# A hybrid encoder layer on one core: the second k tile's modulation on VectorE, statistics ahead of normalising, and the first gating later in the program

## The chip, the cores and the metric

The kernel runs on one core of a Trainium2 chip. The metric is the device time of one execution in microseconds; of the kernel before, three runs gave a median of 936.51 us (934.34 to 937.18). The engines are named as in the profile: PE is TensorE, DVE is VectorE, ACT is ScalarE, POOL is GpSimd, SP is SyncE, which here only issues transfers. PEld is TensorE's loading of weights, which runs beside its products.

## The reference

One layer (DEPTH 1, batch 1, 512 tokens, width 2048). A conditioning vector gives shift, scale and gate; the normalised stream is modulated, projected once onto 7168 columns, and the columns feed a spatial gating group and a neighbourhood attention group:

```python
mod = jax.nn.silu(c) @ w_ada[l] + b_ada[l]
shift, scale, gate = jnp.split(mod[:, None, :], 3, axis=-1)
h = _layernorm(x) * (1.0 + scale) + shift
proj = h @ w_in[l]
u, v, z_a, q, k, v_b, z_b = jnp.split(proj, IN_SPLITS, axis=-1)
y_a = _spatial_gating(gelu(u), gelu(v), z_a, ...)      # u * (W_s LN(v) + b) * silu(z_a)
y_b = _neighbourhood_attention(q, k, v_b, rpb) * silu(z_b)
y = jnp.concatenate([y_a, y_b], axis=-1) @ w_out[l]
x = _layernorm(DEEPNORM_ALPHA * x + (1.0 + gate) * y, ln_g[l], ln_b[l])
```

The gating normalises v in groups of 128 channels, multiplies by a gain and adds a bias per channel, mixes the 128 positions of each chunk with W_s, adds a bias, and multiplies by u and silu(z_a).

## The kernel before

**Products.** Every float32 product is made of three products of rounded parts: the activations are split into h_hi and h_lo, the weights into whi and wlo (`mm3`, L224; `mm_vz`, L237). ACT makes the high part of a weight tile (`L194`), and DVE or POOL subtracts it from the raw tile to get the low part (`L196`); which of the two engines does it is the last field of an entry of the plan (`plan_group`). Weight tiles are read ahead on SP's queue through four raw buffers.

**The start.** The 512 tokens are four tiles of 128 rows (xt). For each, DVE takes statistics (`bn_stats`, `bn_aggr`, L428, L429), POOL makes the factor of the normalisation (L430 to L433), then the four quarters of 512 columns are normalised (L437 on ACT, L440 on POOL or DVE), TensorE transposes each (L444) and ACT copies it back (L445). In the list `LASTS` the fourth tile's quarters stand between the steps of the modulation. The width of 2048 is 16 k tiles of 128. A k tile can be used in products when its shift and scale (modc) are known. For k tiles 0 and 1 these come from TensorE, 32 one-column products each (`ada_tensor`, L348), and DVE adds the bias (L352). For the other 14, in pairs, DVE runs through the weights with a multiply-add into PSUM (`ada_vector`, L363 and L365; acc_ps holds the sums), one addition joins the two halves (L371), and TensorE sums over the partitions with a column of ones (`ada_end`, L379, L380). `make_h` then makes h_hi (ACT, L392) and h_lo (DVE, L393, L397).

**The first part of the projection** is done in segments of k tiles while the modulation proceeds; each segment goes through five groups of columns: VZ0 (first quarter of v_b and z_b), V, U, ZA (half of v, u and z_a) and KQ0. Four banks of PSUM stay with VZ0 throughout; the others are emptied into sums in SBUF (`sum_evac`). The last segment (`last_segment`, k tiles 12 to 15) goes in the order of its list, KQ0, V, U, VZ0, ZA, and empties each group on DVE (L755), with a Gelu or Silu on ACT (L759, L762) and, for ZA, one more product on DVE (L760).

**The first gating** (`sgu`) runs beside the last segment: `run(main, side, pace, start)` takes steps of `side` between the steps of `main`, one for every `pace` steps from step `start` on, and the rest at the end. Its steps for each of four tiles of v are: statistics (L547, L548), the inverse root on POOL (`rsqrt_var`, L120 and L121); then the normalisation on DVE (L552) and two multiplications or additions of 128x512 on POOL (L554, L555). Four steps with TensorE products (L561) and two DVE operations (L562, L565) follow. Its gain, bias, W_s and b_s are loaded on ACT's queue into the four quarters of y_b[1].

**After it** come three groups (qi = 1 to 3) of quarters of v_b, z_b, k and q (`project`, four banks turning with a fifth), each with the attention of the quarter before it as its side (`PACES`), whose scores and values use the PSUM ring "x". v_lo (L688) is made where an attention begins; values (L680 to L682) need the low parts of L710. gate1, which holds the gate later, is filled with zeros by POOL (L530) and its bias loaded ahead of the gating.

**What sets the order** is the order in which instructions are recorded, arranged by a scheduler engine by engine; on each engine it is fixed.

Of the kernel before, what the change touches and what calls it, by code (L numbers as in the profile page):

```python
# [1 line left out]

# [13 lines left out]
P = 128  # L16
D = 2048
T = 512
# [19 lines left out]
            ([4, 5], [VZ0, V, U, ZA, KQ0]), ([6, 7], [KQ0, V, U, VZ0, ZA])]  # L38
# [8 lines left out]
PACE_FIRST = (1.5, 19)  # L47
PACES = [(1.2, 2.95), (1.2, 3.15), (1.2, 3.3), (1.2, 3.15)]
# [11 lines left out]
def run(main, side, pace=1, start=0):  # L60
# [5 lines left out]
    for _ in side:  # L66
        pass
# [3 lines left out]
def hybrid_kernel(ctx: ExitStack, tc: tile.TileContext, x, c, w_ada, b_ada_cols, b_gate, w_in,  # L71
# [235 lines left out]

    with tc.tile_pool(name="ph1", bufs=1) as ph1:
# [65 lines left out]
        def ada_end(k0):

            pc = bank()[:, :4].rearrange("p (s k) -> p s k", s=2)
            for s in range(2):
                for i in range(2):
                    nc.tensor.matmul(pc[:, s, i:i + 1], lhsT=scratch[1][:, (2 * s + i) * P:(2 * s + i + 1) * P], rhs=one, start=True, stop=True)  # L379
            nc.vector.tensor_tensor(out=modc[:, :, k0:k0 + 2], in0=pc, in1=bada[:, :, k0:k0 + 2], op=ALU.add)  # L380
# [37 lines left out]
        nb = ph1.tile([P, NT], F32, name="nb")  # L418
# [4 lines left out]
        def first_norm(n):  # L423

            xn = xt[:, n, :]
            st = ph1.tile([P, 4, 6], F32, name="st", tag="st", bufs=2)
            for i in range(4):
                nc.vector.bn_stats(out=st[:, i, :], in_=xn[:, i * 512:(i + 1) * 512])  # L428
            nc.vector.bn_aggr(out=mv[:, n, :], in_=st)  # L429
            nc.gpsimd.tensor_scalar(out=mv[:, n, 0:1], in0=mv[:, n, 0:1], scalar1=-1.0, scalar2=0.0, op0=ALU.mult, op1=ALU.add)  # L430
            nc.gpsimd.tensor_scalar(out=rstd[:, n:n + 1], in0=mv[:, n, 1:2], scalar1=1.0, scalar2=EPS, op0=ALU.mult, op1=ALU.add)
            nc.gpsimd.tensor_tensor(out=rstd[:, n:n + 1], in0=rstd[:, n:n + 1], in1=mhalf[:, 0:1], op=ALU.pow)
            nc.gpsimd.tensor_scalar(out=nb[:, n:n + 1], in0=mv[:, n, 0:1], scalar1=rstd[:, n:n + 1], scalar2=0.0, op0=ALU.mult, op1=ALU.add)  # L433
            for q in range(4):
                cs = slice(q * T, (q + 1) * T)
                if q == 1:
# [548 lines left out]
```

## Time and profile before

| what | value |
|---|---|
| median of three runs | 936.51 us (934.34 to 937.18) |
| the profiled execution, its span | 936.44 us, 934.7 us |
| busy share PE, DVE, ACT, POOL | 95%, 64%, 35%, 36% |
| mean granted TensorE clock | 0.976 of full |

The span is the time from the first to the last instruction in the profile; the profiled execution's own time is 1.74 us longer. A row of a timeline gives the start, the time that the group of equal instructions took, the engine, the line of the kernel, the operation and the tiles; an entry in square brackets is the time the engine stood idle before it and what ended the wait.

### The profile page before, as it was taken

To read this page: it belongs to the slowest core of one execution; us is meant where nothing else is said; L and a number is where in the kernel's file an instruction comes from. 1 tells how busy PE (TensorE), PEld (TensorE's weight loads), DVE (VectorE), ACT (ScalarE), POOL (GpSimd) and SP (SyncE) were. 2 spreads that over 40 slices of the span, in tenths; PEclk is the share of its full clock that TensorE was granted. 3 is DMA by queue.
4 is the path that set the end of the run, shared out by engine and by line. 5 is a ranking of instruction groups with operands and counts; after the bars stand their busy time and mean duration, and the time that the engine had idled before them with its cause. 6 is when DMAs were issued, how large, how long until landed. Compare 5 with 4: busy or idle time off the path is not lost.

```text
span 934.7 us, 11916 instructions
## 1 busy us (share of the span) xinstructions
PE 890.4 (95%) x4528; PEld 775.7 (83%) x4528; DVE 596.9 (64%) x827; ACT 324.0 (35%) x401; POOL 339.0 (36%) x246
## 2 busy tenths in 40 slices
PE   3899899999997999999999999999999999999993
PEld 3888688888886898899889988999888888888883
DVE  5055898854485544686759686877868835252667
ACT  4235333322614152543345153625154511212300
POOL 4235554635573241615261624253256000000035
PEclk9679999999998999999999999999999999999997
DMA  9778888853422332344543554543333292323213
GB/s 301 220 242 289 276 295 263 292 168 124 143 72 90 91 100 77 117 135 122 176 152 121 164 167 138 158 152 122 113 111 112 91 353 97 113 92 112 90 60 121
DMA packets 107787, 145.59 MB, mean 156 GB/s; under 512 B 6994, under 2 KB 78802, under 8 KB 106962
## 3 DMA queue, kind: packets, MB, share of 16 engines
q1 hardware_dynamic: 103120, 134.25, 45.1%
q10 hardware_dynamic: 4610, 10.59, 3.2%
q8 instruction: 35, 0.57, 0.3%
q14 instruction: 22, 0.17, 0.1%
HBM read 140.62 MB, written 4.19 MB: 155 GB/s over the span
## 4 chain that ended last, share of the span: by engine, by line
PE 82%; POOL 4%; DVE 4%; issue 4%; DMA 3%; SPq 1%; ACT 1%; POOLq 0%; DVEq 0%; ACTq 0%
PE psm L224 52%; PE psx L224 15%; PE psm L237 8%; DMA wada<-in_w_ada_dram 2%; SPq L320 1%; POOL wlo L196 1%; PE ada L348 1%; POOL xr L864 1%; DVE s L552 1%; PE psx L682 1%; PE psx L634 1%; PE psx L633 1%; PE psx L680 1%; DMA xt<-in_x_dram 1%; POOL xr L865 1%
## 5 line engine op out<-in xcount | busy, mean ns | idle before, releaser
L194 ACT CAST whi<-raw 128x1024 fp32r<-128x1024 f32 x133 | 139.2, 1049 | 337.5 <-PE psm L224 216.9
L196 DVE TENSOR_TENSOR wlo<-raw,whi 128x1024 fp32r<-128x1024 f32 x94 | 131.4, 1399 | 160.8 <-ACT whi L194 155.2
L224 PE MATMUL psm<-h_hi,whi 128*128 128x512 f32 x444 | 175.1, 395 | 0.0
L224 PE MATMUL psm<-h_lo,whi 128*128 128x512 f32 x444 | 173.7, 391 | 0.0
L224 PE MATMUL psm<-h_hi,wlo 128*128 128x512 f32 x444 | 173.2, 390 | 0.0
L196 POOL TENSOR_TENSOR wlo<-raw,whi 128x1024 fp32r<-128x1024 f32 x39 | 95.0, 2443 | 107.4 <-ACT whi L194 83.8
L224 PE MATMUL psm<-whi,h_hi 128*128 128x512 f32 (+1 forms) x296 | 114.7, 388 | 0.0
L224 PE MATMUL psm<-wlo,h_hi 128*128 128x512 f32 (+1 forms) x296 | 114.0, 385 | 0.0
L224 PE MATMUL psm<-whi,h_lo 128*128 128x512 f32 (+1 forms) x296 | 114.0, 385 | 0.0
L224 PEld LDWEIGHTS psm<-h_hi,wlo 128*128 128x128 f32 x444 | 83.3, 188 | 17.8
L224 PEld LDWEIGHTS psm<-h_hi,whi 128*128 128x128 f32 x444 | 84.0, 189 | 15.2
L224 PEld LDWEIGHTS psm<-h_lo,whi 128*128 128x128 f32 x444 | 83.9, 189 | 15.1
L237 PE MATMUL psm<-whi,h_hi 128*128 128x256 f32 x248 | 71.4, 289 | 4.0 <-ACT whi L194 2.1
L237 PE MATMUL psm<-wlo,h_hi 128*128 128x256 f32 x248 | 71.3, 288 | 0.2 <-POOL wlo L196 0.2
L121 POOL TENSOR_TENSOR rs<-vareps,mhalf 128x1 f32<-128x1 f32 x4 | 4.4, 1098 | 184.4 <-DVE vareps L120 184.4
L237 PE MATMUL psm<-whi,h_lo 128*128 128x256 f32 x248 | 70.9, 287 | 0.1
L224 PEld LDWEIGHTS psm<-wlo,h_hi 128*128 128x128 f32 x296 | 63.6, 215 | 8.5
L224 PEld LDWEIGHTS psm<-whi,h_lo 128*128 128x128 f32 x296 | 63.4, 214 | 8.5
L224 PEld LDWEIGHTS psm<-whi,h_hi 128*128 128x128 f32 x296 | 63.4, 214 | 8.4
L365 DVE SCALAR_TENSOR_TENSOR ada<-wada,c_sb,ada 128x512 f32<-128x512 f32 x91 | 64.0, 749 | 7.4 <-DMA wada<-in_w_ada_dram 3.9
L224 PE MATMUL psx<-h_hi,whi 128*128 128x512 f32 x160 | 64.5, 403 | 4.1 <-ACT whi L194 2.2
L224 PE MATMUL psx<-h_hi,wlo 128*128 128x512 f32 x160 | 63.5, 397 | 2.9 <-POOL wlo L196 2.9
(199 smaller groups left out, 1679.6 us busy)
## 6 DMA issues: line engine op xcount, KB each, us to landing
wada<-in_w_ada_dram SPq DMA_DIRECT2D x128, 256.0 KB, 5.5
raw<-in_w_in_dram SPq DMA_DIRECT2D x128, 256.0 KB, 3.2
raw<-in_w_in_dram SPq DMA_DIRECT2D x48, 512.0 KB, 4.2
rawg<-in_w_ada_dram SPq DMA_DIRECT2D x32, 512.0 KB, 4.1
raw<-in_w_out_dram SPq DMA_DIRECT2D x32, 512.0 KB, 3.6
xt<-in_x_dram SPq DMA_DIRECT2D x8, 512.0 KB, 8.6
xr<-in_x_dram ACTq DMA_DIRECT2D x4, 1024.0 KB, 9.4
tt<-in_rpb_dram ACTq DMA_DIRECT2D x16, 128.0 KB, 2.9
```

What stands on the lines that cost most here:

```text
L194: nc.scalar.copy(out=hi, in_=raw)
L196: eng.tensor_tensor(out=low, in0=raw, in1=hi.bitcast(F32), op=ALU.subtract)
L224: nc.tensor.matmul(ps, lhsT=a, rhs=b, start=first and j == 0, stop=last and j == 2)
L237: nc.tensor.matmul(ps[:, t * w:(t + 1) * w], lhsT=a, rhs=b[:, cs], start=first and t == 0 and j == 0, stop=last and t == 1 and j == 2)
L320: nc.sync.dma_start(out=wt[:, :, s, :], in_=w_ada_v[:, j0:j0 + step, s * D + k0 * P:s * D + k0 * P + w])
L348: nc.tensor.matmul(pc[s], lhsT=wt[:, j - j0, s, :], rhs=c_sb[:, j:j + 1], start=j == 0, stop=j == NK - 1)
L365: nc.vector.scalar_tensor_tensor(out=even if j == NK - 2 else acc, in0=wt[:, j - j0], scalar=cj, in1=acc, op0=ALU.mult, op1=ALU.add)
L552: nc.vector.tensor_scalar(out=v[n][:, tok(g)], in0=v[n][:, tok(g)], scalar1=mvs[:, g, 0:1], scalar2=rs[:, g:g + 1], op0=ALU.subtract, op1= ...
L633: nc.tensor.matmul(po, lhsT=k2[:, h, keys], rhs=q2[:, h, q], start=True, stop=False)
L634: nc.tensor.matmul(po, lhsT=klo[:, h, keys], rhs=q2[:, h, q], start=False, stop=True)
L680: nc.tensor.matmul(ps[:, q], lhsT=v_hi[:, t, h, :], rhs=hi[:, sl], start=t == 0, stop=False, skip_group_check=True)
L682: nc.tensor.matmul(ps[:, q], lhsT=v_hi[:, t, h, :], rhs=lo[:, sl], start=False, stop=t == 3, skip_group_check=True)
```

## The change

The second k tile's modulation (`ada_vector(1, 1)`) moves from TensorE to DVE, in operations of 128x256, with one product pair to sum over the partitions; the first weight tile's low part is DVE's. The statistics of a tile go ahead of the normalisation of the tile before it, and the quarters are normalised by POOL, and by DVE for the third and fourth tile's even quarters; none by ACT. The last segment goes KQ0, U, V, VZ0, ZA; the gating's first steps start at step 24 of the segment at a pace of 1.7, and what is left of it when the segment ends goes into the next group ahead of the attention, together with the filling of gate1. The gating's loads go into the quarters of gate1. The first attention's pace is (1.05, 1).

```diff
-            ([4, 5], [VZ0, V, U, ZA, KQ0]), ([6, 7], [KQ0, V, U, VZ0, ZA])]
+            ([4, 5], [VZ0, V, U, ZA, KQ0]), ([6, 7], [KQ0, U, V, VZ0, ZA])]
...
-PACE_FIRST = (1.5, 19)
-PACES = [(1.2, 2.95), (1.2, 3.15), (1.2, 3.3), (1.2, 3.15)]
+PACE_FIRST = (1.7, 24)
+PACES = [(1.05, 1), (1.2, 3.15), (1.2, 3.3), (1.2, 3.15)]
...
-            plan_group(w_in_v, firsts[q], [2 * pair for pair in pairs], "pool")
+            plan_group(w_in_v, firsts[q], [2 * pair for pair in pairs], "pool" if plan else "dve")
...
-        def ada_vector(k0, before):
-
-            even, both = scratch[:2]
-            for j0 in range(0, NK, 2):
+        def ada_vector(k0, nk, before=()):
+
+            w, step = nk * P, 4 // nk
+            even, both = [t[:, :2 * w].rearrange("p (s w) -> p s w", s=2) for t in scratch[:2]]
+            accs = [t[:, :2 * w].rearrange("p (s w) -> p s w", s=2) for t in acc_ps]
+            for j0 in range(0, NK, step):
                 wt = ada_next()
-                for j in range(j0, j0 + 2):
-                    cj, acc = c_sb[:, j:j + 1], acc_ps[j % 2]
+                for j in range(j0, j0 + step):
+                    cj, acc = c_sb[:, j:j + 1], accs[j % 2]
...
         def prepare():
-            for kk in range(2):
-                yield from ada_tensor(kk)
-                make_h(kk, True)
-                yield
+            yield from ada_tensor(0)
+            make_h(0, True)
+            yield
+            yield from ada_vector(1, 1)
+            yield from ada_end(1, 1)
...
+        def normalise(n):
+
+            xn = xt[:, n, :]
             for q in range(4):
                 cs = slice(q * T, (q + 1) * T)
-                if q == 1:
-                    nc.scalar.activation(out=xn[:, cs], in_=xn[:, cs], func=AF.Identity, scale=rstd[:, n:n + 1], bias=nb[:, n:n + 1])
-                else:
-                    eng = nc.vector if q == 2 or q == 3 == n else nc.gpsimd
-                    eng.tensor_scalar(out=xn[:, cs], in0=xn[:, cs], scalar1=mv[:, n, 0:1], scalar2=rstd[:, n:n + 1],
-                                      op0=ALU.add, op1=ALU.mult)
+                eng = nc.vector if n >= 2 and q % 2 == 0 else nc.gpsimd
+                eng.tensor_scalar(out=xn[:, cs], in0=xn[:, cs], scalar1=mv[:, n, 0:1], scalar2=rstd[:, n:n + 1],
+                                  op0=ALU.subtract, op1=ALU.mult)
...
+        for n in range(NT):
+            statistics(n)
+            if n:
+                for _ in normalise(n - 1):
+                    pass
+            inverse(n)
+        lasts = normalise(NT - 1)
...
-    run(last_segment(), sgu(0, acc_v, y_a0, *y_b[1], y_b[0][3], "m"), *PACE_FIRST)
+    def gating():
+
+        yield from sgu(0, acc_v, y_a0, *scratch, y_b[0][3])
+        nc.gpsimd.memset(gate1, 0.0)
+        nc.scalar.dma_start(out=gate1[0:1, :], in_=b_gate)
+
+    first_gating = gating()
+    run(last_segment(), first_gating, *PACE_FIRST, finish=False)
...
         side = attention(qi - 1, kq, vb)
+        if qi == 1:
+            side = chain(first_gating, side)
```

In the order of TensorE before, behind the first half of the first weights' products (psm and psx are the PSUM banks of VZ0 and V), the modulation of k tile 1 begins (ada is the PSUM tile with its columns):

```order
L224 MATMUL psx<-whi,h_hi 128x512
L224 MATMUL psx<-wlo,h_hi 128x512
L224 MATMUL psx<-whi,h_lo 128x512
L348 MATMUL ada_111<-c_sb,wada 128x1
L348 MATMUL ada_112<-c_sb,wada 128x1
```

In the same place of the changed kernel TensorE has two products with a column of ones (gate_89 is where VectorE's sums were left), and the products of the second half follow:

```order
L225 MATMUL psx<-whi,h_hi 128x512
L225 MATMUL psx<-wlo,h_hi 128x512
L225 MATMUL psx<-whi,h_lo 128x512
L383 MATMUL ada_111<-one,gate_89 128x1 x2
L238 MATMUL psm<-whi,h_hi 128x256
L238 MATMUL psm<-wlo,h_hi 128x256
```

The 32 one-column products of k tile 1 left TensorE's order. VectorE's order before, from the end of k tile 1's modulation to the pair of k tiles 2 and 3:

```order
L352 TENSOR_TENSOR modc<-ada_111,bada 128x1
L352 TENSOR_TENSOR modc<-ada_112,bada 128x1
L393 TENSOR_SCALAR xt<-xt,modc 128x4x128
L397 TENSOR_TENSOR h_lo<-xt,h_hi 128x512
L363 TENSOR_SCALAR ada_111<-wada,c_sb 128x512
L363 TENSOR_SCALAR ada_112<-wada,c_sb 128x512
L365 SCALAR_TENSOR_TENSOR ada_111<-wada,c_sb,ada_111 128x512
```

VectorE's order after, from the end of k tile 0's modulation to the first operations of k tile 1's:

```order
L354 TENSOR_TENSOR modc<-ada_111,bada 128x1
L354 TENSOR_TENSOR modc<-ada_112,bada 128x1
L397 TENSOR_SCALAR xt<-xt,modc 128x4x128
L401 TENSOR_TENSOR h_lo<-xt,h_hi 128x512
L197 TENSOR_TENSOR wlo<-raw,whi 128x1024
L367 TENSOR_SCALAR ada_111<-wada,c_sb 128x256
L367 TENSOR_SCALAR ada_112<-wada,c_sb 128x256
L369 SCALAR_TENSOR_TENSOR ada_111<-wada,c_sb,ada_111 128x256
L369 SCALAR_TENSOR_TENSOR ada_112<-wada,c_sb,ada_112 128x256
```

The first low part and 16 operations of half the width now stand between k tile 0's h_lo and the pair's. At the end of the last segment, VectorE's order before, from the gating's last normalisation (s is a tile of v, y_a_93 the sum of U) into the gating's products:

```order
L552 TENSOR_SCALAR s<-s,mvs,rss 128x128
L755 TENSOR_TENSOR y_a_93<-psx,y_a_93 128x512
L688 TENSOR_TENSOR v_lo<-vb,v_hi 128x1024
L196 TENSOR_TENSOR wlo<-raw,whi 128x1024
L562 TENSOR_TENSOR y_b_104<-psm,y_b_105 128x512
L565 TENSOR_TENSOR y_a_93<-y_b_104,y_a_93 128x4x128
```

The same place after, where s in L760 is a sum of ZA:

```order
L553 BN_AGGR mvs<-sts 128x2 x2
L121 TENSOR_SCALAR vareps<-mvs 128x4
L557 TENSOR_SCALAR s<-s,mvs,rss 128x128 x4
L693 TENSOR_TENSOR v_lo<-vb,v_hi 128x1024
L197 TENSOR_TENSOR wlo<-raw,whi 128x1024 x2
L760 TENSOR_TENSOR s<-psx,s 128x512 x2
L765 TENSOR_TENSOR y_a_93<-y_a_93,s 128x512
L760 TENSOR_TENSOR s<-psx,s 128x512
```

ZA's sums now stand behind the last normalisation, v_lo and two low parts. POOL's order before at the gating's end (y_b1_105 holds the gain and the bias; the last two rows are the low parts of the last weights of ZA's products):

```order
L121 TENSOR_TENSOR rss_2318<-vareps_2328,mhalf_85 128x4
L555 TENSOR_TENSOR s_98<-s_98,y_b1_105 128x512
L554 TENSOR_TENSOR s_98<-s_98,y_b1_105 128x512
L555 TENSOR_TENSOR s_98<-s_98,y_b1_105 128x512
L196 TENSOR_TENSOR wlo_2219<-raw_2109,whi_2218 128x1024
L196 TENSOR_TENSOR wlo_2288<-raw_2139,whi_2287 128x1024
```

POOL's order after, in the same place (gate1_89 holds the gain and the bias; wlo_2223 is the low part of ZA's second weights):

```order
L560 TENSOR_TENSOR s_97<-s_97,gate1_89 128x512
L559 TENSOR_TENSOR s_98<-s_98,gate1_89 128x512
L197 TENSOR_TENSOR wlo_2223<-raw_2114,whi_2222 128x1024
L560 TENSOR_TENSOR s_98<-s_98,gate1_89 128x512
L122 TENSOR_TENSOR rss_2342<-vareps_2352,mhalf_85 128x4
L559 TENSOR_TENSOR s_98<-s_98,gate1_89 128x512
L560 TENSOR_TENSOR s_98<-s_98,gate1_89 128x512
L773 MEMSET gate1_89 128x2048
```

ZA's second low part now stands inside the gating's POOL work, and the filling of gate1 behind it.

## Rows read from the trace of the kernel before

**Rows 1.** The page's busy time: us, share of the span, instructions.

```profile
PE 890.4 (95%) x4528; PEld 775.7 (83%) x4528; DVE 596.9 (64%) x827; ACT 324.0 (35%) x401; POOL 339.0 (36%) x246
```

**Rows 2.** Stretches of the span: its bounds, its length, busy time (and instructions) of PE, PEld, DVE, ACT and POOL, the granted clock of TensorE, the share of the DMA engines, GB/s.

```profile
44.67:52.45 7.78, 7.78 (x58) 7.78 (x57) 0.00 (x0) 0.00 (x0) 0.00 (x0) 0.80 0.51 151
52.45:55.22 2.77, 1.67 (x9) 1.59 (x9) 0.34 (x3) 0.87 (x2) 0.00 (x0) 0.50 0.51 153
...
60.00:110.00 50.00, 47.45 (x219) 39.84 (x219) 33.58 (x51) 25.18 (x38) 24.95 (x12) 1.00 0.93 304
...
235.00:286.00 51.00, 45.64 (x219) 39.88 (x219) 31.32 (x74) 25.03 (x34) 33.74 (x22) 0.99 0.33 98
286.00:312.00 26.00, 25.18 (x135) 21.85 (x136) 17.20 (x21) 8.52 (x11) 3.18 (x1) 0.89 0.34 101
...
325.00:800.00 475.00, 475.00 (x2478) 416.16 (x2477) 326.46 (x412) 184.29 (x221) 168.69 (x128) 1.00 0.44 140
```

**Rows 3.** TensorE's list of waits: engine, line and tile that waited, what it waited for, us in total, times, the longest.

```profile
PE psm L444 <- POOL xt L440: 14.8, 4, 12.0
...
PE psx L224 <- POOL wlo L196: 2.9, 1, 2.9
PE psx L224 <- ACT whi L194: 2.2, 1, 2.2
```

**Rows 4.** The timeline of the start, all engines: start, us, engine, line, operation, tiles, count, and in brackets the idle time before it and its releaser.

```profile
37.76 0.69 DVE L397 TENSOR_TENSOR h_lo<-xt,h_hi 128x512 fp32r<-128x512 f32 x1
...
38.09 4.93 POOL L196 TENSOR_TENSOR wlo<-raw,whi 128x1024 fp32r<-128x1024 f32 x2 [14.30 <-ACT whi L194]
...
44.67 9.45 PE L348 MATMUL ada<-c_sb,wada 128*128 128x1 f32 x64
46.54 11.64 SPq L320 DMA_DIRECT2D wada<-in_w_ada_dram  x9
52.45 0.16 DVE L352 TENSOR_TENSOR modc<-ada,bada 128x1 f32<-128x1 f32 x1 [14.00 <-PE ada L348]
54.16 0.16 DVE L352 TENSOR_TENSOR modc<-ada,bada 128x1 f32<-128x1 f32 x1 [1.55 <-PE ada L348]
54.35 0.81 ACT L392 ACTIVATE h_hi<-xt,modc 128x512 fp32r<-128x512 f32 x1 [15.40 <-DVE modc L352]
...
55.22 0.28 PEld L237 LDWEIGHTS psm<-whi,h_hi 128*128 128x128 f32 x1 [1.18 <-ACT h_hi L392]
...
56.39 1.40 DVE L363 TENSOR_SCALAR ada<-wada,c_sb 128x512 f32<-128x512 f32 x2
```

**Rows 5.** Groups of instructions on DVE by form: line, operation, tiles, shapes, count, busy us, mean ns of one, idle time before them.

```profile
L365 DVE SCALAR_TENSOR_TENSOR ada<-wada,c_sb,ada 128x512 f32<-128x512 f32 x91 | 64.0, 749 | 7.4 <-DMA wada<-in_w_ada_dram 3.9 <-issue 3.2
...
L363 DVE TENSOR_SCALAR ada<-wada,c_sb 128x512 f32<-128x512 f32 x14 | 9.9, 746 | 0.0
...
L755 DVE TENSOR_TENSOR s<-psx,s 128x512 f32<-128x512 f32 x8 | 5.4, 688 | 3.2 <-PE psx L224 3.2
...
L380 DVE TENSOR_TENSOR modc<-psx,bada 128x4 f32<-128x4 f32 x7 | 1.1, 164 | 12.1 <-PE psx L379 11.9
```

**Rows 6.** The timeline during the first gating, DVE and POOL.

```profile
258.80 2.40 POOL L196 TENSOR_TENSOR wlo<-raw,whi 128x1024 fp32r<-128x1024 f32 x1 [2.20 <-ACT whi L194]
258.96 2.27 DVE L120 TENSOR_SCALAR vareps<-mvs 128x4 f32<-128x4 f32 x1
...
261.30 1.03 POOL L121 TENSOR_TENSOR rss<-vareps,mhalf 128x4 f32<-128x4 f32 x1
262.37 1.12 DVE L552 TENSOR_SCALAR s<-s,mvs,rss 128x128 f32<-128x128 f32 x4 [0.36 <-POOL rss L121]
...
263.57 1.29 POOL L554 TENSOR_TENSOR s<-s,y_b 128x512 f32<-128x512 f32 x1 [1.23 <-DVE s L552]
...
265.94 1.29 POOL L555 TENSOR_TENSOR s<-s,y_b 128x512 f32<-128x512 f32 x1
266.01 2.07 DVE L552 TENSOR_SCALAR s<-s,mvs,rss 128x128 f32<-128x128 f32 x4 [0.80 <-POOL rss L121]
```

**Rows 7.** TensorE's timeline in the last segment: the first product of VZ0, the last one, the first of ZA, and the first that needs ZA's low part.

```profile
268.32 0.28 PE L237 MATMUL psm<-whi,h_hi 128*128 128x256 f32 x1
...
279.59 0.39 PE L224 MATMUL psm<-h_hi,wlo 128*128 128x512 f32 x1
282.21 0.50 PE L224 MATMUL psx<-h_hi,whi 128*128 128x512 f32 x1 [2.24 <-ACT whi L194]
...
285.88 0.79 PE L224 MATMUL psx<-h_hi,wlo 128*128 128x512 f32 x1 [2.93 <-POOL wlo L196]
```

**Rows 8.** The timeline at the end of the gating, all engines: POOL's two low parts, v_lo, and a low part on DVE.

```profile
283.48 5.70 POOL L196 TENSOR_TENSOR wlo<-raw,whi 128x1024 fp32r<-128x1024 f32 x2
...
285.71 1.22 DVE L688 TENSOR_TENSOR v_lo<-vb,v_hi 128x1024 fp32r<-128x1024 f32 x1 [4.29 <-ACT v_hi L687]
...
289.04 1.23 DVE L196 TENSOR_TENSOR wlo<-raw,whi 128x1024 fp32r<-128x1024 f32 x1 [2.11 <-ACT whi L194]
```

**Rows 9.** The first attention: the products of scores and values on TensorE in 318 to 350 us (line, count, ns shortest, median and longest, first and last start), and POOL's low parts of the probabilities in the timeline.

```profile
L634 PE MATMUL psx<-q,klo x4: 273/278/281, 320.4 to 322.5; 128*128 128x192 f32 x2, 128*128 128x256 f32 x2
L680 PE MATMUL psx<-hi,v_hi x2: 253/279/305, 349.4 to 349.7; 128*128 128x192 f32 x1, 128*128 128x256 f32 x1
...
340.17 4.23 POOL L710 TENSOR_TENSOR s<-s,hi 128x896 fp32r<-128x896 f32 x2 [1.06 <-ACT hi L708]
```

More of the change, by code (lines that the diff above doesn't have):

```diff
@@ L1 @@
 from contextlib import ExitStack
+from itertools import chain
 import concourse.bass as bass
@@ L57, with run @@
 SLOTS = [0, 192, 448, 704, 896]
-def run(main, side, pace=1, start=0):
+def run(main, side, pace=1, start=0, finish=True):
     for i, _ in enumerate(main):
@@ L65, in run @@
                 next(side, None)
-    for _ in side:
+    for _ in side if finish else ():
         pass
@@ L306, in hybrid_kernel @@
     accs = {V: (acc_v, False), U: (y_a0, True), ZA: (acc_z, True), KQ0: (y_b[1], True)}
+    scratch = [gate1[:, i * T:(i + 1) * T] for i in range(4)]
     with tc.tile_pool(name="ph1", bufs=1) as ph1:
@@ L370, in ada_vector, with ada_end @@
                     yield from before
-            nc.vector.tensor_tensor(out=both, in0=acc_ps[1], in1=even, op=ALU.add)
-            yield
[L374 to L380, printed above, removed]
-            yield
-            for kk in range(k0, k0 + 2):
-                make_h(kk)
+            nc.vector.tensor_tensor(out=both, in0=accs[1], in1=even, op=ALU.add)
+        def ada_end(k0, nk):
+            pc = acc_ps[0][:, T - 2:] if nk == 1 else bank()[:, :4]
+            pc = pc.rearrange("p (s k) -> p s k", s=2)
+            for s in range(2):
+                for i in range(nk):
+                    nc.tensor.matmul(pc[:, s, i:i + 1], lhsT=scratch[1][:, (nk * s + i) * P:(nk * s + i + 1) * P], rhs=one, start=True, stop=True)
+            nc.vector.tensor_tensor(out=modc[:, :, k0:k0 + nk], in0=pc, in1=bada[:, :, k0:k0 + nk], op=ALU.add)
+            yield
+            for kk in range(k0, k0 + nk):
+                make_h(kk, nk == 1)
                 yield
@@ L446, in first_norm @@
                 yield
-        for n in range(NT - 1):
-            for _ in first_norm(n):
-                pass
-        lasts = first_norm(NT - 1)
+        for n in range(NT):
[5 more added lines that the diff above has]
+        lasts = normalise(NT - 1)
         for what in LASTS:
@@ L529, in hybrid_kernel, with sgu @@
     rings["x"][0] = ps_x.enter_context(tc.tile_pool(name="ps_x1", bufs=4, space=PSUM))
-    nc.gpsimd.memset(gate1, 0.0)
-    nc.scalar.dma_start(out=gate1[0:1, :], in_=b_gate)
-    def sgu(half, v, y, gB, bB, wsT, bs, sv, ring="x"):
+    def sgu(half, v, y, gB, bB, wsT, bs, sv):
         hs = slice(half * 512, (half + 1) * 512)
@@ L558, in sgu @@
         for g in range(4):
-            ps = bank(ring)
+            ps = bank()
             for n in range(4):
```

20 lines of the change are left out of this document (8 added, 12 removed).

## The prediction

> **What bounds the kernel now.** First the page's busy shares: TensorE computes for 890.4 us of the 934.7 us span [rows 1], so a change can only win back what TensorE loses by standing still, by running at its lower clock, or by work that is no product. The table of stretches tells where that is [rows 2]. From 325 to 800 us TensorE is busy for 475.00 of 475 us at granted clock 1.00, and nothing is to be had there. At the start, 44.67 to 52.45 us is counted as fully busy, but that is the second k tile's modulation; the products stand still. Around the first gating, 235 to 286 us has 45.64 of 51.00 us and 286 to 312 us has 25.18 of 26.00 us at a granted clock of 0.89. Then the list of waits names the releasers [rows 3]: the transposes wait 14.8 us for the normalised stream, and the pauses at the gating end on a POOL low part (2.9 us) and an ACT high part (2.2 us). Last, the timelines of the two places [rows 4, 7, 8].
>
> **Change 1, the second k tile's modulation.** Before, TensorE has 64 records of one column in 9.45 us, from 44.67 us; modc at 54.16, h_hi at 54.35, the next product at 55.22 us [rows 4]. TensorE's queue is in order, so the other half of these weights' products stands behind them. VectorE ends its h_lo at 37.76 + 0.69 = 38.45 us and stands idle until 52.45 us [rows 4]. The new work on VectorE in its order: one low part, 1.23 us beside nothing [rows 8], to 39.68; 16 operations of 128x256; one combination; after two TensorE products the modc. No row has 128x256 with a PSUM operand. The nearest are 0.749 us at 512 columns, and the additions from PSUM of 0.688 us at 512 and 0.164 us at 4 [rows 5]: straight between the last two is 0.42 us at 256, a slope of 1.03 ns a column. The 512-column form, run back to back, starts every 0.65 us (two of 0.746 took 1.40 in all [rows 4, 5]); less 256 x 1.03 ns = 0.26 it starts every 0.40 us. From both sides: 0.33 (half of 0.65) and 0.65 (no gain from halving). I take 0.40: 16 x 0.40 = 6.4, to 46.1; combination 0.42, to 46.5; two products and modc, some 0.65, to 47.15; and from modc to TensorE's next product 55.22 - 54.16 = 1.06 as before. TensorE goes on at 48.2 instead of 55.22, **7.0 us earlier**; at 0.33 it is 8.1, at 0.65 it is 3.0. [...]
>
> How much of 7.0 lasts? The weights of the next modulation wait for free slots; the first such DMA issue stands at 46.54 us, and TensorE frees the slots [rows 4]. Now VectorE frees the first at 39.68 + 1.6 = 41.3 us, 5.2 us earlier, the last about 7.6 earlier. DMA share is 0.93 in 60 to 110 us, and TensorE loses 2.55 us there [rows 2]; that stretch can only move as far as the transfers do. I keep **6.5 us**, bounds 2.5 and 8.
>
> The first low part on VectorE instead of POOL: POOL took 4.93 us for two, and TensorE's low-part product came when the first was ready [rows 4]; it is inside the gap just worked out, at most 0.4 us, and I count nothing.
>
> **Change 2, statistics ahead.** Twelve quarters on POOL instead of seven plus four on ACT: TensorE's first modulation starts with the stream's weights and transposes interleaved, and only the last tile's chain counts (the 14.8 us of waits lie mostly ahead of it, the longest single one 12.0 [rows 3]). POOL drops eight small operations and gains five quarters; VectorE no longer waits between the tiles. The two cancel within about 1 us either way: zero, bounds -1 and +1.
>
> **Change 3, the gating.** What is lost now: 5.36 us idle in 235 to 286, 0.82 in 286 to 312, and 11% of 26 us by clock, 2.86 [rows 2]: **9.0 us**. By the rows: VZ0 ends at 279.98, ZA waits for its high part until 282.21, its low part until 285.88 [rows 7], as POOL came to that low part only at 283.48, behind the gating's last multiplications [rows 8].
>
> After: with U ahead of V the four tiles reach the gating later, while VZ0 and ZA remain. Let V end at 0. VZ0 takes 279.98 - 268.32 = 11.7 us [rows 7]; ZA, 48 products at 0.23, 11; ZA's second weights are wanted at 11.7 + 5.5 = 17.2. POOL's queue up to their low part: three powers at 1.03, two low parts at 2.40, five multiplications at 1.29 (together 14.35), and the first statistics 1.05. VectorE's normalisations of 1.12 cannot run beside a POOL operation: one took 2.07 beside a multiplication, the vareps of 4 columns 2.27 beside a low part [rows 6]. Three of them alternate with POOL's: 3.4. Sum 18.8, a wait of **1.6 us**. POOL goes on with a multiplication, the fourth power and the fourth normalisation, 3.4, to 22.2. Behind that in VectorE's order stand v_lo (1.22), two low parts of the next group (1.23 each) and only then ZA's sums out of PSUM. Before, ZA's sums came after one low part, with the gating long over. If POOL's last two multiplications alternate with them, the first low part is there at 22.2 + 1.22 + 1.29 + 1.23 = 25.9 and TensorE, at 23.8 + 0.5, waits **1.6 us**; the second at 28.5; four sums and two products at 0.69 with the Silu between bring the last sum to about 33, and only that frees the second PSUM bank of the next group, wanted some 1.5 us after 25.9: **5.5 us**. [...] Idle 8.7 or 6.1, plus the slow restart of the kind seen now, 2.86: 9.0 to 11.6, mean **10.3 against 9.0: 1.3 us lost**, bounds -6 (below) and +9.
>
> [...]
>
> The four products, the filling of gate1 and the one load of the gate's bias behind it move into the next group: TensorE's part is the same, and POOL has little to do there (3.18 of 26 us in 286 to 312 [rows 2]). The gating's four loads on ACT's queue now go into gate1 instead of y_b[1] and can be issued no later than before; the weights' loads keep their order on SP. All of that costs nothing as long as that room lasts, and the filling's own time on POOL if it doesn't. The attention's first values come 12 products of 0.23 earlier, 2.8 us, against the last scores: those stand at 322.5, the low parts end at 340.17 + 4.23 = 344.40 and the first values come at 349.4 [rows 9], a cushion of 5.0 us. Nothing; without cushion 2.8.
>
> **Sum.** 936.44 (the profiled execution; the median of the runs, 936.51, is 0.07 from it) - 6.5 + 0 + 1.3 = **931.2 us**.
>
> **Rivals.** (a) *The later gating pays.* U's products now run while POOL does nothing for the gating, and if VectorE runs its queue without alternation and the ZA sums come at 27 rather than 33, only the wait of 1.6 and half the clock loss remain, 3.0 of 9.0: 936.44 - 6.5 - 6.0 = 923.9. For it: the two pauses named in rows 3 both come from POOL and ACT being late for ZA, and that cause goes. Against: three VectorE operations stand ahead of the sums. (b) *Half-width operations cost as whole ones.* Sixteen at 0.65 are 10.4; TensorE restarts at 52.2, and 2.5 is kept: 936.44 - 2.5 + 1.3 = 935.2. For it: 0.164 us for 4 columns shows a fixed part [rows 5]; against: the fixed part is small. (c) *Slower.* The boundary behind V blocks VectorE further: the filling of gate1, or the Silu's table, falls into its queue, and the ZA sums come at 41 instead of 33. Each us that the last sum is later is a us of TensorE. From about 38 on the boundary costs more than the start gains (9.0 + 6.5 = 15.5 lost in all); at 41 it is 19: 936.44 - 6.5 + 10 = 939.9. For it: POOL and VectorE each waited at the same place [rows 6, 8]; against: the last step needs 8 us that no queued operation accounts for. (d) *The modulation wasn't the bound.* If the weights of these tiles arrive no sooner, the restart at 48.2 only opens idle time before 110 us: 936.44 - 1 + 1.3 = 936.7. Against: TensorE was busy for 47.45 of the 50 us behind it [rows 2].
>
> **How the numbers follow.** Forecast 0.50, (a) 0.18, (b) 0.14, (c) 0.11, (d) 0.07. A measurement of this kernel tells 0.3%, 2.8 us, from no change: faster ends at 933.7, slower begins at 939.3. The forecast's own range is 928 to 935, nine tenths of it faster; (a) is faster; (b) is a quarter faster, the rest within; (c) is three quarters slower; (d) is within, with a tenth slower. Faster 0.45 + 0.18 + 0.03 = 0.66; slower 0.08 + 0.01 = 0.09; within 0.25. The range leaves out half of (a)'s low side and most of (c)'s high side: 924 to 938.5.
>
> **What would show it.** Right: VectorE has 16 operations of 0.4 us from 39.7 us, TensorE's first product behind them at 47 to 49, and the wait list has a line of a few us on VectorE's ZA sum at the head of the next group, with low clock after it. Wrong: restart past 51 (b); no idle time over 3 us between VZ0 and the next group (a); a single idle of over 10 us there (c); or 60 to 110 us with more than 6 us of TensorE idle (d).

## The result

The changed kernel is slower: 947.22 us (945.11 to 948.39, four runs) against 936.3 us (934.34 to 937.18, four runs), a ratio of 1.0117 with a 95% interval of 1.0092 to 1.0142. The forecast was 931.2 us in a range of 924 to 938.5, so it was wrong, and on the wrong side. None of the rivals covers it either: (c) had the loss at the gating, and it will turn out to lie at the start.

The page of the changed kernel's profile, part 1 (busy time, share of the span, instructions):

```profile
span 946.2 us, 11802 instructions
PE 891.0 (94%) x4468; PEld 773.6 (82%) x4468; DVE 603.9 (64%) x843; ACT 321.6 (34%) x397; POOL 354.1 (37%) x242
```

TensorE does the same work as in [rows 1] (891.0 against 890.4 us) in a span that is 11.5 us longer; POOL is 15.1 us busier (354.1 against 339.0), with four instructions fewer. That is the first hint: some of POOL's operations became dearer. TensorE's list of waits (engine, line, tile, what was waited for, us in total, times, longest):

```profile
PE psm L448 <- POOL xt L444: 21.2, 9, 12.6
PE psm L238 <- DVE s L760: 4.9, 1, 4.9
PE psm L238 <- DVE h_lo L401: 4.6, 2, 3.6
...
PE psx L225 <- DVE y_b L475: 2.0, 2, 1.1
PE psx L225 <- POOL wlo L197: 1.3, 1, 1.3
PE psx L225 <- ACT gate L472: 1.2, 1, 1.2
...
PE psm L238 <- DVE wlo L197: 0.2, 1, 0.2
```

The first line is the one of [rows 3] with 14.8 us in 4 waits; it is now nine waits. POOL's timeline at the start shows why (start, us, engine, line, operation, tiles, count, idle time before):

```profile
10.46 8.25 POOL L444 TENSOR_SCALAR xt<-xt,mv,rstd 128x512 f32<-128x512 f32 x4
...
34.67 4.40 POOL L444 TENSOR_SCALAR xt<-xt,mv,rstd 128x512 f32<-128x512 f32 x2
```

Four quarters take 8.25 us, 2.07 each, and the last ends at 34.67 + 4.40 = 39.07 us. The kernel before has an operation of the same name on the same tile, 128x512 with two scalars from a tile, and POOL did two of them in 1.51 us, with the last one ending at 23.79 (its timeline, not among the rows above):

```profile
11.20 1.51 POOL L440 TENSOR_SCALAR xt<-xt,mv,rstd 128x512 f32<-128x512 f32 x2
...
22.72 1.07 POOL L440 TENSOR_SCALAR xt<-xt,mv,rstd 128x512 f32<-128x512 f32 x1
```

What follows at the start is as the sum had it, only late. VectorE's and TensorE's timelines of the changed kernel, where the second k tile is modulated:

```profile
54.92 0.87 DVE L367 TENSOR_SCALAR ada<-wada,c_sb 128x256 f32<-128x256 f32 x2
55.69 4.79 DVE L369 SCALAR_TENSOR_TENSOR ada<-wada,c_sb,ada 128x256 f32<-128x256 f32 x12
...
61.30 0.42 DVE L375 TENSOR_TENSOR gate<-ada,gate 128x256 f32<-128x256 f32 x1
62.42 0.16 DVE L384 TENSOR_TENSOR modc<-ada,bada 128x2 f32<-128x2 f32 x1 [0.70 <-PE ada L383]
```

```profile
63.49 0.58 PE L238 MATMUL psm<-whi,h_hi 128*128 128x256 f32 x1 [1.10 <-ACT h_hi L396]
```

TensorE takes up the products at 63.49 us, where [rows 4] have 55.22: 8.3 us late instead of 7.0 early. Some 3 us more go before the gating (POOL's first pair of low parts in the last segment's second group starts at 263.22 instead of 251.82 us, 11.4 later), and behind that the balance hardly changes: the span's end is 11.5 us later. The attention's long stretch is full, as before ([rows 2]'s last row):

```profile
336.00:811.00 475.00, 474.57 (x2475) 415.51 (x2474) 324.60 (x412) 183.58 (x220) 167.83 (x128) 1.00 0.44 140
```

The 3 us between the restart and 263.22 can be read from the lists of waits. In these 199.73 us of the changed kernel TensorE stands still for 8.1 us: for VectorE's h_lo 4.6, for the sums in y_b 2.0, for ACT's copies into gate1 1.2, for modc 0.3. In the 196.60 us of the kernel before, from 55.22 to 251.82, it is 5.7: for sums 3.1 and 1.6, a copy 0.7, modc 0.3. That is 2.4 us of the 3.1; the other 0.7 is that the products themselves took longer, with a granted clock of 0.50 from 63.49 to 73.00 us, against 0.55 from 55.22 to 60.00 before. Ahead of both TensorE had largely stood still (busy for 1.74 of the 3.99 us up to 63.49, and for 1.67 of 2.77 up to 55.22 [rows 2]). One of the two waits for h_lo is here (VectorE's timeline, then POOL's):

```profile
64.96 2.40 DVE L401 TENSOR_TENSOR h_lo<-xt,h_hi 128x512 fp32r<-128x512 f32 x1
```

```profile
64.45 2.37 POOL L197 TENSOR_TENSOR xlo<-raw,xhi 128x1024 fp32r<-128x1024 f32 x1 [4.87 <-DMA wada<-in_w_ada_dram]
```

An operation of 0.69 us [rows 4] takes 2.40 beside a low part of POOL that has begun half a us before it. The wait for ACT's copy is taken up under change 3.

### The profile page after: what moved, and what is told of

It is laid out like the page before. It is cut to its first block, busy times and chain, and to the rows that moved or that the text cites. A ratio compares the mean times of both kernels' runs of the same rounds, so it can differ in the third digit from the quotient of the medians.

```text
span 946.2 us, 11802 instructions
## 1 busy us (share of the span) xinstructions
PE 891.0 (94%) x4468; PEld 773.6 (82%) x4468; DVE 603.9 (64%) x843; ACT 321.6 (34%) x397; POOL 354.1 (37%) x242
## 4 chain that ended last, share of the span: by engine, by line
PE 81%; POOL 7%; DVE 5%; issue 3%; DMA 2%; ACT 1%; POOLq 0%; SPq 0%; ACTq 0%; DVEq 0%
PE psm L225 52%; PE psx L225 14%; PE psm L238 8%; POOL xt L444 2%; PE ada L350 1%; POOL wlo L197 1%; POOL xr L878 1%; DVE ada L369 1%; DMA raw<-in_w_in_dram 1%; PE psx L687 1%; PE psx L639 1%; PE psx L566 1%; PE psx L638 1%; PE psx L685 1%; POOL xr L879 1%
## 5 line engine op out<-in xcount | busy, mean ns | idle before, releaser
L197 POOL TENSOR_TENSOR wlo<-raw,whi 128x1024 fp32r<-128x1024 f32 x38 | 91.6, 2416 | 114.7 <-ACT whi L195 82.2
L369 DVE SCALAR_TENSOR_TENSOR ada<-wada,c_sb,ada 128x512 f32<-128x512 f32 (+1 forms) x104 | 69.1, 715 | 2.1 <-DMA wada<-in_w_ada_dram 1.8
```

Source lines behind the costliest of these rows:

```text
L197: eng.tensor_tensor(out=low, in0=raw, in1=hi.bitcast(F32), op=ALU.subtract)
L369: nc.vector.scalar_tensor_tensor(out=even if j == NK - 2 else acc, in0=wt[:, j - j0], scalar=cj, in1=acc, op0=ALU.mult, op1=ALU.add)
```

## The experiments

The theory after the result (A): the diff turns the normalisation's `op0=ALU.add` on a negated mean into `op0=ALU.subtract` on the mean itself, and on POOL that form is dear. The rival (B): it is the new arrangement, twelve quarters in a row on POOL with VectorE's statistics beside them. The first four kernels tell them apart and price the other two parts alone. Below, kernel 1 is the kernel of experiment 1, and so on.

**1. The changed kernel with ADD.**

```diff
         def inverse(n):
+            nc.gpsimd.tensor_scalar(out=mv[:, n, 0:1], in0=mv[:, n, 0:1], scalar1=-1.0, scalar2=0.0, op0=ALU.mult, op1=ALU.add)
...
-                                  op0=ALU.subtract, op1=ALU.mult)
+                                  op0=ALU.add, op1=ALU.mult)
```

> The changed kernel, with the mean negated by a small POOL operation as before and the quarters normalised by ADD and MULT instead of SUBTRACT and MULT. Theory A (the form of the POOL operation sets its price): POOL's quarters fall from 2.07 us to 0.76 each, the last ends at 24 to 25 us instead of 39, TensorE's first product behind the second modulation stands near 48 instead of 63, and the time is 930 to 933 us. Theory B (twelve quarters in a row on POOL, or VectorE's statistics beside them, make each slow): they stay at 2.07 and the time stays at 945 to 948 us.

Measured: 931.11 us (929.14 to 934.26), ratio to the kernel before 0.9955 (0.9931 to 0.9978). POOL's timeline of it:

```profile
10.97 3.02 POOL L445 TENSOR_SCALAR xt<-xt,mv,rstd 128x512 f32<-128x512 f32 x4
...
22.89 1.94 POOL L445 TENSOR_SCALAR xt<-xt,mv,rstd 128x512 f32<-128x512 f32 x2
```

Four in a row now take 3.02 us, 0.76 each, with the same arrangement and the same statistics beside them; the last ends at 24.83 us. TensorE takes up the products at 47.13 us. So the form of this one operation cost 947.2 - 931.1 = 16.1 us, and (B) falls.

**2. The kernel before with SUBTRACT.**

```diff
-            nc.gpsimd.tensor_scalar(out=mv[:, n, 0:1], in0=mv[:, n, 0:1], scalar1=-1.0, scalar2=0.0, op0=ALU.mult, op1=ALU.add)
...
-                                      op0=ALU.add, op1=ALU.mult)
+                                      op0=ALU.subtract, op1=ALU.mult)
```

(ACT's bias is multiplied by -1 in place of an added zero.)

> The kernel before, with the mean not negated, and the quarters of POOL and VectorE normalised by SUBTRACT and MULT. Theory A: POOL's seven quarters take 2.07 us each instead of 0.76, VectorE's stay at 0.55; POOL needs 5.2 to 5.4 us a tile, the last quarter ends near 29 us instead of 23.8, and the time is 939 to 942 us. Theory B: they stay at 0.76 and the time stays at 936 us.

Measured: 946.01 us (944.17 to 946.65), ratio 1.0111 (1.0078 to 1.0143). POOL's group of quarters in it (count, busy us, mean ns):

```profile
L439 POOL TENSOR_SCALAR xt<-xt,mv,rstd 128x512 f32<-128x512 f32 x7 | 14.8, 2115 | 0.0
```

The seven quarters take 2.1 us each in the old arrangement as well. The price is as expected, and the last quarter ends at 28.07 + 2.38 = 30.5 us, 6.7 late; the time rose by 9.8 us where 3 to 6 were expected. In the profiled execution all of it is there when the second modulation begins on TensorE, at 52.52 us against 44.67 in [rows 4], 7.9 later; its span is 7.7 us longer (942.4 against 934.7). Most of the rest of the 9.8 is that the profiled execution is the fastest of the four: it took 944.17 us, 1.8 less than the median, at a mean granted clock of 0.974; the other three had 0.969 or 0.970.

**3. The modulation alone.** The kernel before with `ada_tensor`, `ada_vector`, `ada_end` and `prepare` of the changed kernel, and the first low part on VectorE:

```diff
-            yield from ada_tensor(kk)
...
+            yield from ada_tensor(0)
+            make_h(0, True)
+            yield
+            yield from ada_vector(1, 1)
+            yield from ada_end(1, 1)
```

> The kernel before with the second k tile's modulation on VectorE and the first low part there, nothing else. Neither theory on POOL touches it. If the sum's term holds (7.0 us earlier at the restart, 6.5 kept): TensorE goes on at 48 us and the time is 929 to 931 us. If transfers or the low parts behind it give the shift back: 933 to 936 us.

Measured: 926.75 us (926.53 to 928.9), ratio 0.9913 (0.9881 to 0.9945): 9.45 us gained, more than the 7.0 of the restart. VectorE's and then TensorE's timeline of it:

```profile
35.11 0.16 DVE L352 TENSOR_TENSOR modc<-ada,bada 128x1 f32<-128x1 f32 x1 [0.27 <-PE ada L348]
...
39.38 4.79 DVE L367 SCALAR_TENSOR_TENSOR ada<-wada,c_sb,ada 128x256 f32<-128x256 f32 x12
...
46.11 0.16 DVE L382 TENSOR_TENSOR modc<-ada,bada 128x2 f32<-128x2 f32 x1 [0.70 <-PE ada L381]
```

```profile
47.18 0.58 PE L237 MATMUL psm<-whi,h_hi 128*128 128x256 f32 x1 [1.10 <-ACT h_hi L394]
```

Sixteen operations of half the width take 6.4 us (38.61 to 44.99, where the combination starts; 0.40 each, as estimated). The restart is at 47.18, 8.0 us earlier; one of them comes from k tile 0's modulation, ready at 35.11 instead of 36.01 us: `ada_tensor` of the changed kernel also pins the order of its one-column products, which no run changes alone. And the shift grows behind the restart instead of shrinking. The stretch that was feared:

```profile
60.00:110.00 50.00, 48.62 (x239) 41.31 (x239) 37.25 (x54) 22.31 (x32) 26.89 (x13) 1.00 0.95 308
```

TensorE is busy for 48.62 us of it instead of 47.45 [rows 2], at a DMA share of 0.95. The modc of the second pair comes 25.56 us after that of the first, at 95.38 after 69.82, where the kernel before has 28.46 (105.17 after 76.71): the transfers moved forward with the slots.

**4. The gating alone.** The kernel before with the last segment's order, `PACE_FIRST`, `PACES[0]`, the loads into gate1 and `gating()` of the changed kernel, and its modulation and normalising as they were:

```diff
-            ([4, 5], [VZ0, V, U, ZA, KQ0]), ([6, 7], [KQ0, V, U, VZ0, ZA])]
+            ([4, 5], [VZ0, V, U, ZA, KQ0]), ([6, 7], [KQ0, U, V, VZ0, ZA])]
...
-    run(last_segment(), sgu(0, acc_v, y_a0, *y_b[1], y_b[0][3], "m"), *PACE_FIRST)
+    first_gating = gating()
+    run(last_segment(), first_gating, *PACE_FIRST, finish=False)
```

> The kernel before with the last segment's order, the gating's place and the first attention's pace of the changed kernel, and nothing else. The sum's term was +1.3 us: 937 to 939 us, with TensorE waiting 3 to 6 us for VectorE's ZA sum. Rival: what the gating costs at its new place equals what it cost at the old one, 935 to 937 us. If the rise of 11 us came from here, 944 us or more.

Measured: 939.09 us (937.44 to 941.92, ten runs), ratio 1.0036 (1.0020 to 1.0053): 2.9 us lost. TensorE's list of waits of it:

```profile
PE psm L238 <- DVE s L754: 4.9, 1, 4.9
...
PE psx L225 <- POOL wlo L197: 1.2, 1, 1.2
PE psx L225 <- ACT gate L466: 1.2, 1, 1.2
```

The two waits of [rows 3] on POOL's low part and ACT's high part (2.9 and 2.2) are gone, and one of 4.9 on VectorE's sum of ZA and one of 1.2 on ZA's low part stand in their place; the last line is far ahead of the gating. The profiled execution, 937.59 us, is one of the fastest of the ten: its span is 1.2 us longer than that of the kernel before, and 1.0 of them are there when the second group of the last segment begins on POOL (252.86 against 251.82 us). In the changed kernel the wait for ZA's sum is the same 4.9. Its cause in the changed kernel, VectorE's and POOL's timelines:

```profile
300.48 1.11 DVE L557 TENSOR_SCALAR s<-s,mvs,rss 128x128 f32<-128x128 f32 x4 [4.57 <-POOL rss L122]
301.51 1.22 DVE L693 TENSOR_TENSOR v_lo<-vb,v_hi 128x1024 fp32r<-128x1024 f32 x1
302.64 2.35 DVE L197 TENSOR_TENSOR wlo<-raw,whi 128x1024 fp32r<-128x1024 f32 x2
304.91 1.28 DVE L760 TENSOR_TENSOR s<-psx,s 128x512 f32<-128x512 f32 x2
```

```profile
301.67 4.45 POOL L559 TENSOR_TENSOR s<-s,gate 128x512 f32<-128x512 f32 x1 [1.23 <-DVE s L557]
```

VectorE waited 4.57 us for POOL's fourth power, and the sums of ZA stand behind the normalisation, v_lo and two low parts. POOL's multiplication, which takes 1.29 us elsewhere [rows 6], took 4.45: VectorE went through v_lo and the two low parts, to 304.99 us, and POOL came last.

**5. Modulation, and statistics ahead with ADD; gating as before.** Kernel 3 with `statistics`, `inverse` and `normalise` of kernel 1.

> The kernel before with the modulation on VectorE and the statistics ahead of normalising, but with the mean negated and ADD; gating as before. Theory A: only the form of the POOL operation was at fault, and the new distribution over the engines is worth nothing either way: the last quarter ends at 24.5 to 25 us and the time is 926 to 929 us, beside 926.75 of the modulation alone. Rival: twelve quarters on POOL cost something of their own: 930 us or more.

Measured: 924.93 us (923.54 to 927.01), ratio 0.9885 (0.9860 to 0.9910). The new arrangement costs nothing when its operations have the old form, and it may gain: 1.8 us below kernel 3, but the intervals overlap, so that is not settled. Kernel 1, which differs from it by the moved gating with its order and paces alone, is 6.2 us slower. That is not lost at the gating: of the 7.9 us between the two profiled spans, 7.1 are there when the second group of the last segment begins on POOL (247.47 against 240.36 us). Where they come from stands under change 3.

**6. Four forms on POOL in one kernel.** The kernel before, with its seven quarters written in different forms on lines of their own (one run; its time says nothing):

```diff
+                    elif (n, q) == (0, 3):
+                        nc.gpsimd.tensor_scalar(out=xn[:, cs], in0=xn[:, cs], scalar1=m, scalar2=g, op0=ALU.subtract, op1=ALU.mult)
+                    elif (n, q) == (1, 0):
+                        nc.gpsimd.tensor_scalar(out=xn[:, cs], in0=xn[:, cs], scalar1=g, scalar2=u, op0=ALU.mult, op1=ALU.add)
+                    elif (n, q) == (1, 3):
+                        nc.gpsimd.tensor_scalar(out=xn[:, cs], in0=xn[:, cs], scalar1=g, scalar2=v, op0=ALU.mult, op1=ALU.subtract)
```

> The kernel before with the seven POOL quarters in different forms, each on its own line: ADD then MULT, SUBTRACT then MULT, MULT then ADD, MULT then SUBTRACT at 512 columns, and the first two in halves of 256. Theory A1 (SUBTRACT anywhere in the two-step operation is slow): MULT-ADD 0.76 us, SUBTRACT-MULT and MULT-SUBTRACT 2.07. Theory A2 (only SUBTRACT as the first step, with a scalar from a tile, is slow): MULT-SUBTRACT 0.76. Theory A3 (a fixed cost of some 1.3 us per operation): SUBTRACT-MULT at 256 takes 1.7; if it is a price per column it takes 1.05 to 1.1, and ADD-MULT at 256 some 0.4. The time itself says nothing, 936 to 940 us.

Measured, in POOL's timeline (ADD-MULT, SUBTRACT-MULT, MULT-ADD, MULT-SUBTRACT, and the first two in halves):

```profile
11.40 0.76 POOL L457 TENSOR_SCALAR xt<-xt,nm,rstd 128x512 f32<-128x512 f32 x1
12.15 2.07 POOL L445 TENSOR_SCALAR xt<-xt,mv,rstd 128x512 f32<-128x512 f32 x1
...
16.16 0.76 POOL L447 TENSOR_SCALAR xt<-xt,rstd,nb 128x512 f32<-128x512 f32 x1
16.91 2.07 POOL L449 TENSOR_SCALAR xt<-xt,rstd,pb 128x512 f32<-128x512 f32 x1
...
20.65 1.09 POOL L452 TENSOR_SCALAR xt<-xt,nm,rstd 128x256 f32<-128x256 f32 x2
21.72 2.43 POOL L455 TENSOR_SCALAR xt<-xt,mv,rstd 128x256 f32<-128x256 f32 x2
```

SUBTRACT is dear as the first and as the second step (A1; one instruction of each form here, beside the seven of kernel 2 and the twelve of the changed kernel). It is mostly a price per column: at half the width it takes 1.22 instead of 2.07 us, so 0.85 us for 256 columns, 3.3 ns each, where ADD has 0.55 and 0.76, 0.8 ns each. (The halves ran beside VectorE's work, and in the same run one ADD quarter took 1.06, so the smaller difference is the less certain.) On VectorE the form makes no difference: its five SUBTRACT quarters in this kernel take 0.546 us, and the ADD quarters of the kernel before took 0.547.

**7. Kernel 1 with ZA's low parts on VectorE.**

```diff
-            plan_group(w_in_v, firsts[q], [2 * pair for pair in pairs], "pool" if plan else "dve")
+            plan_group(w_in_v, firsts[q], [2 * pair for pair in pairs], "dve" if not plan or (q == ZA and pairs == [6, 7]) else "pool")
```

> The changed kernel with ADD, and ZA's two low parts of the last segment on VectorE instead of POOL. Theory G1 (POOL's chain decides when the last normalisation and so VectorE's ZA sums come): the chain is 2.4 us shorter twice, the wait of 4.9 us for the ZA sum falls to 0 to 2.5 and the time is 926 to 929 us, beside 931.1. Theory G2 (VectorE's own queue decides): the two low parts, 1.23 us each, make VectorE's queue longer; the wait stays at 4 to 7 us and the time at 930 to 933 us.

Measured: 928.06 us (927.45 to 928.51), ratio 0.9914 (0.9897 to 0.9930). TensorE's list of waits and POOL's timeline:

```profile
PE psm L238 <- DVE s L761: 4.3, 1, 4.3
```

```profile
282.26 4.40 POOL L560 TENSOR_TENSOR s<-s,gate 128x512 f32<-128x512 f32 x1 [1.29 <-DVE s L558]
```

The time is the one that G1 named, 3 us lower; the wait is the one that G2 named. POOL's chain is shorter (from V's first sum to the start of the last normalisation it is 22.2 us, in the changed kernel 24.8) and the 1.3 us wait for ZA's low part is gone, and the sum that TensorE waits for comes 2.6 us earlier than in the changed kernel (counted from V's first sum). But TensorE comes to it 2.1 us earlier too, so the wait stays: VectorE's queue behind the last normalisation still ends after TensorE's products.

**8. Kernel 3 with ZA's low parts on VectorE**, the same edit, gating as before.

> The kernel before with the modulation on VectorE, the gating as before, and ZA's two low parts of the last segment on VectorE instead of POOL. If ZA's low part was late only because it stood behind the gating's multiplications in POOL's queue: the wait of 2.9 us goes, part of the low clock behind it goes too, and the time is 921 to 924 us beside 926.75. If VectorE is held up by POOL's last multiplications there: 926 to 928 us.

Measured: 924.13 us (921.69 to 924.57), ratio 0.9867 (0.9846 to 0.9887). That is 2.6 us below kernel 3, though the two intervals just overlap. The wait of 2.9 us for POOL's low part has become one of 0.5 for VectorE's:

```profile
PE psx L224 <- ACT whi L194: 2.2, 1, 2.2
...
PE psx L224 <- DVE wlo L196: 0.5, 1, 0.5
```

**9. Kernels 5 and 8 together.** Modulation on VectorE, statistics ahead with ADD, ZA's low parts on VectorE, the gating as before.

> The kernel before with the modulation on VectorE, the statistics ahead of normalising with ADD, the gating as before, and ZA's two low parts of the last segment on VectorE. If the three gains are of different places they add: 926.75 less 1.8 for the statistics and less 2.6 for the low parts, 922 to 923 us. If the second only moves what the first had already freed: 924 to 926 us.

Measured: 923.46 us (921.45 to 928.31), the kernel before beside it 934.34; ratio 0.9884 (0.9851 to 0.9918). Against its own comparison that is the same as kernels 5 (0.9885) and 8 (0.9867): all three are some 11 to 12 us faster than the kernel before, and that the two smaller gains add is not shown.

## Why the prediction was wrong

**The step that failed is change 2, "The two cancel within about 1 us either way: zero, bounds -1 and +1".** It counted POOL's operations (eight small ones fewer, five quarters more) and let a quarter keep its price. The diff has the line in which `op0` goes from add to subtract, and the step passed over it as the same instruction. Seven quarters, mostly at 0.76 us, became twelve at 2.07 or more: the last quarter ends at 39.07 us instead of 23.79, 15.3 us later, and kernel 1 gives the whole as 16.1 us. The trace of before has no SUBTRACT of two steps on POOL, so its price had to be bounded from both sides by the nearest rows, as was done for the half-width operations of change 1, and it wasn't. A row of POOL's subtractions was near: the low part, 2.40 us for 1024 columns [rows 6], 1.2 for 512, though with two tensors. Twelve at that price would have been 5 us more than at 0.76, and the bounds would at least have had the right sign.

**Change 1 was right in kind and too small.** 16 x 0.40 = 6.4 us measured 6.4, the combination 0.42 as estimated. The restart gained 8.0 instead of 7.0, and what is kept is 9.45 us (kernel 3) instead of 6.5: the term "that stretch can only move as far as the transfers do" was mis-sized, since the transfers moved with the slots that VectorE frees. In the changed kernel none of it could show, as everything waited for POOL's quarters.

**Change 3 was right in sign, and wrong in place.** Kernel 4 lost 2.9 us alone (1.9 to 5.0 by its interval) where 1.3 was put down. But the gating's new place costs almost nothing against the old one. From POOL's first low parts in the last segment's second group on, 73.18 us hold nearly the same products; here is that stretch in the kernel before and in the changed one:

```profile
251.82:325.00 73.18, 67.19 (x369) 58.87 (x369) 45.95 (x88) 24.11 (x30) 32.70 (x22) 0.95 0.30 88
```

```profile
263.22:336.40 73.18, 66.81 (x371) 60.49 (x370) 43.99 (x89) 24.14 (x30) 35.92 (x24) 0.95 0.28 82
```

TensorE is idle for 6.0 us before and 6.4 after, at the same granted clock, and from the start of this stretch to the end of the span it is 682.88 and 682.98 us (683.04 in kernel 4). The single waits of the changed kernel: ZA's low part 1.3 (1.6 expected), the next group's 0.2 (1.6), the sum of ZA 4.9 (5.5), 6.4 in all. That is the lower of the two idle times that the prediction took the mean of, 8.7 and 6.1: 9.0 with the clock, the 9.0 of before. The 2.6 us between the two are an estimate that no run shows by itself; in its place the runs showed VectorE going through v_lo and two low parts in a row while POOL's multiplication of 1.29 us took 4.45. So the step that failed at the gating is the strict alternation, and the mean of 10.3 taken with it.

What the moved gating did cost lies 80 us and more ahead of it, in a term that the prediction put at nothing: "The gating's four loads on ACT's queue now go into gate1 instead of y_b[1] and can be issued no later than before". They are issued earlier, and that is what hurts. W_s goes into the third quarter of gate1, which still serves as scratch for ZA's partial sums. The changed kernel's timelines of POOL, ACT and TensorE:

```profile
174.41 3.78 POOL L473 TENSOR_TENSOR s<-gate,s 128x512 f32<-128x512 f32 x3
```

```profile
178.22 0.33 ACTq L545 DMA_DIRECT2D gate<-in_w_sp_dram  x1
178.60 0.59 ACT L472 COPY gate<-psx 128x512 f32<-128x512 f32 x1 [2.27 <-POOL s L473]
```

```profile
179.24 0.50 PE L225 MATMUL psx<-h_hi,xhi 128*128 128x512 f32 x1 [1.20 <-ACT gate L472]
```

The load goes out when POOL's third addition has ended, at 178.19 us; ACT's copy of the next partial sum stands behind it in the queue, and TensorE waits 1.20 us for the bank. The same wait of 1.2 us is in the lists of kernels 1, 4 and 7, and in none that leaves the gating as before (3, 5, 8 and 9), where this load goes out some 80 us later (252.06 us in the kernel before, 169.70 in kernel 4). In the changed kernel and in kernels 1 and 7 VectorE's next two h_lo then come behind a wait for weights (2.8, 2.1 and 2.3 us, in kernel 5 1.2) and beside a low part of POOL, and TensorE waits for them for another 3.6, 2.9 and 3.1 us, in kernel 5 for 0.3. Of the 7.1 us that kernel 1 loses to kernel 5 ahead of the gating, 5.1 come here: it is 2.0 us behind at one modc (144.31 against 142.35) and 7.0 at the second one after it (197.31 against 190.29). That the loads are the cause is read from these traces; no run puts them back alone.

Of VectorE and POOL beside each other, the traces show two things. VectorE kept going through three operations while POOL's one of 1.29 us took 4.45; and yet VectorE's normalisation waited out a POOL low part that had begun (3.18 us instead of 1.12), as the changed kernel's two timelines have it:

```profile
281.83 3.18 DVE L557 TENSOR_SCALAR s<-s,mvs,rss 128x128 f32<-128x128 f32 x4 [0.83 <-POOL rss L122]
```

```profile
281.76 2.39 POOL L197 TENSOR_TENSOR wlo<-raw,whi 128x1024 fp32r<-128x1024 f32 x1
```

In these two places the POOL operation that was running was waited for, to 284.15 us, and the one that came second was passed over while VectorE had the next one ready, to 304.99 us. That the two take turns was the prediction's estimate, and it was wrong.

**The rivals.** (b) is refuted, 0.40 us at half width; (d) too, as kernel 3's gain is kept to the end; (a), the later gating paying, is refuted by kernel 4. (c) is not what happened: the last sum of ZA is out of PSUM at 309.81 us, some 30 us after V (its last sum starts at 279.91), where the forecast had 33 and (c) 41. Kernel 1 lands at 931.1 beside the forecast of 931.2, and that is luck: the terms miss in opposite directions, as the modulation gained 3 more and the moved gating cost 1.6 (kernel 4) to 4.9 (kernel 1 against kernel 5) more.

**Left open.** What the gating's loads cost by themselves, and so what its new place would be worth with the loads in y_b[1]; and whether the statistics ahead of normalising gain anything with ADD (1.8 us, within the intervals).

## What to carry to other kernels

Read a diff for operations that change their form, not only for those that move: here one opcode in a two-step operation changed its price 2.7 times on one engine (0.76 to 2.07 us on POOL) and not at all on another (0.55 us on VectorE), and a form that the trace doesn't show needs its own bounds. On POOL the sign was better moved into the scalar: negating a 128x1 mean costs 0.19 us, and saved 1.3 us on each quarter of 512 columns. Work moved from TensorE onto an idle VectorE was worth what it freed in TensorE's queue and in the transfer slots together, 9.45 us in kernel 3. And when a load gets another buffer, ask who uses that buffer last and what stands behind the load in its queue: here TensorE waited 1.20 us behind a load that was issued earlier.

## What the runs showed of the hardware

- POOL's TENSOR_SCALAR on 128x512 float32: 0.76 us with ADD and MULT in either order, 2.07 us with SUBTRACT as either step (kernel 6); on VectorE 0.55 us with ADD or SUBTRACT ahead of MULT.
- VectorE and POOL did not take turns: POOL's multiplication of 1.29 us took 4.45 us (the changed kernel, kernels 1 and 4) and 4.40 us (kernel 7) beside three VectorE operations in a row, v_lo and two low parts. A POOL low part that had begun was waited out: in the changed kernel VectorE's h_lo of 0.69 us took 2.40 beside one of 2.37, and its normalisation of 1.12 us 3.18 beside one of 2.39.
- In the changed kernel a load on ACT's queue that waited for its buffer held ACT's work behind it: ACT stood idle for 2.27 us ahead of the copy behind the load, and TensorE for 1.20 us.
- VectorE's multiply-adds into PSUM at 128x256 started every 0.40 us (kernel 3, 16 in 6.4 us, two plain multiplications among them), against 0.65 at 128x512 (the kernel before, two of 0.75 in 1.40 us).
